# HGRN2's score products gathered into one column-tiled group, in one core's step of a hybrid retention and HGRN2 layer

## The chip, the cores and the metric

The kernel runs on one core of a Trainium2 chip. The metric is device time in microseconds; a time is the median of the runs.

## What is computed

One step of a decoder layer for two request groups that share weights: 272 prompt tokens (16 learned meta tokens and 256 of the prompt) and 8 single sample tokens with states of their own. D_MODEL is 2048, everything is float32.

```
x <- LN1(alpha*x + 0.5*SwiGLU_1(x))
x <- LN2(alpha*x + Mixer(x))        # retention and HGRN2 side by side, gated, one output projection
x <- LN3(alpha*x + 0.5*SwiGLU_2(x))

def hgrn2_chunk(S, q, k, v, logf):          # 16 heads, 128 state features
    b = cumsum(logf)
    diff = b[:, :, :, None, :] - b[:, :, None, :, :]
    decay = exp(where(causal, diff, -inf))
    A = einsum('bhid,bhjd,bhijd->bhij', q, k, decay)
    o = einsum('bhij,bhjv->bhiv', A, v) + einsum('bhid,bhdv->bhiv', q * exp(b), S)
    S_new = exp(b_last) * S + einsum('bhjd,bhjv->bhdv', k * exp(b_last - b), v)

def retention_chunk(S, q, k, v):            # 8 heads of 256, decay gamma per head
    inner = einsum('bhid,bhjd->bhij', q, k) * D
    o = einsum('bhij,bhjv->bhiv', inner, v) + einsum('bhid,bhdv->bhiv', q_dec, S)
    S_new = gamma**C * S + einsum('bhjd,bhjv->bhdv', k_dec, v)
```

In HGRN2 the decay differs for each feature, so the scores A of a chunk cannot be one plain product q k. The sample tokens take one recurrent step each and need their states (16 heads of 128 x 128 and 8 heads of 256 x 256, for each of 8 tokens) read, updated, queried and written.

## The kernel before

Activations lie transposed: features on the 128 partitions, tokens along the free dimension (280 columns, 264 without the meta tokens). Each weight matrix is streamed from memory in units of eight 128 x 128 blocks (`stream`, L170, with the load on SP's queue at L185). ScalarE casts a unit to `whi` (L188), VectorE makes the rest `wlo` (L189), and `dense` (L218) multiplies each block three times, hi by hi, hi by lo and lo by hi, in one-pass float32. Three buffers each hold `raw`, `whi` and `wlo`.

Between the two feed-forward parts stands the mixer. It runs over eight units u; a unit has two HGRN2 heads and one retention head. Per unit `project` runs ten projections of two output chunks each, 16 contraction blocks per projection, six matmuls per block. After each contraction block it calls `pump`: the two branches are generators, `mix_hg` (HGRN2) and `mix_ret` (retention), each `yield n` says after how many pumps the branch goes on, and so the branch's TensorE instructions are laid between the dense ones in an order written by hand. A branch that started first comes first within one pump. Unit u's `mix_hg` starts when its `i_h` projection is done, `mix_ret` after `v_r`; the first wait is 3 pumps, except in units 0 and 1 (20 and 46 for HGRN2, 24 for retention's unit 1). TensorE keeps that order; the instructions of the other engines and the DMA issues are put in order by a scheduler, which may put them well before the pump at which they are emitted, as far as their operands allow.

HGRN2's scores are built by levels s = 1, 2, 4, ..., 64 (`LEVELS`): at level s, the later half of each block of 2s tokens meets the earlier half. K and Q are scaled in place from level to level (`scale_k`, `scale_q`, and `join` for the products of forget gates `Ts`). Levels 1 to 8 are computed as 32 x 16 pieces (`blocks`, from the side-by-side copies Q1 and Q4 of `side_by_side`) and put into the score tile `acc` by masked copies (L834); the diagonal comes with Q1 as `own` (L828). Levels 16, 32 and 64 have products of their own (L886, L881), copied by ScalarE (L899, L894). All these products use column tiles: 32 or 64 stationary columns at a `tile_position`, so that two or four of them run side by side. A group of them takes one or two PSUM banks out of the four of `ps_m` (`mx_bank`), which also serve the transposes `pt`, `ptk` and the branches' other products.

Before the change there are five such groups per unit, at the yields L858 to L904: Q1 with the diagonal, Q4, 16, 32, 64. After the group of a level, K and Q are scaled for the next one. Q1 and Q4 lie in buffers of the tag `smh`, which the sample states (`sms`, loaded by `load`, L770, behind their broadcast `vbs` in the tag `vbh`) take afterwards. The sample states are updated at L927 and L928, and queried in a column-tiled group `pq` (L954). Retention has its own, `pqr` (L1125), which begins with a third score block of 16 columns (L1056); its first two score blocks, 256 and 144 columns wide, are full-array products into `psc`. Its own state updates are L1106 and L1112.

Of the kernel before, what the change touches and what calls it, by code (L numbers as in the profile page):

```python
# [14 lines left out]
ALU = mybir.AluOpType  # L15
# [3 lines left out]
P = 128  # L19
# [4 lines left out]
NMETA, SEQ, NS = 16, 256, 8  # L24
# [104 lines left out]
def trunk(ctx: ExitStack, tc: tile.TileContext, A, O):  # L129
# [13 lines left out]
    def mx_bank(name):  # L143
        return ps_m.tile([P, 512], F32, tag="mx", name=name)
# [135 lines left out]
    class Norm:  # L280
# [266 lines left out]
    with tc.tile_pool(name="yp", bufs=1) as yp:  # L547
# [7 lines left out]
        with tc.tile_pool(name="mp", bufs=1) as mp:  # L555
# [190 lines left out]
            def mix_hg(u, f, k, q, v):  # L746
# [18 lines left out]
                def load(h):  # L765

                    sms.append(tmp("smh", (P, NS, P), bufs=2))
                    vbs.append(tmp("vbh", (P, NS, P), bufs=2))
                    nc.sync.dma_start(vbs[h], vrow[h].partition_broadcast(P))
                    nc.sync.dma_start(sms[h], A["sg"][2 * u + h])  # L770
# [27 lines left out]

                def side_by_side(s):

                    x = tmp("Qm", (P, 3, 2 * P), tag="smh", bufs=2)
# [3 lines left out]
                    nc.scalar.copy(part(1, 2 * s), odd(2 * s))  # L805
# [5 lines left out]
                def blocks(x, s, own=None):  # L811

                    x = x.rearrange("p i (x j c) -> p i x j c", x=4, j=4)
                    for h in range(2):
                        pl = mx_bank("pl")
                        half = pl[:, : 2 * 80].rearrange("p (b c) -> p b c", b=2)
                        for b in range(2):
                            for mine in range(1 if own is None else 2):
                                for j in range(0, P, 32):
                                    at = b * P + j  # L820
                                    o, y = half[j : j + 32, b, :48].rearrange("p (i c) -> p i c", i=3), x[:, :, 2 * h + b, j // 32, :]
                                    if mine:
                                        o, y = half[j : j + 32, b, 48:], own[:, h, at : at + 32]
                                    nc.tensor.matmul(
                                        o, K[:, h, NMETA + at : NMETA + at + 32], y, start=True, stop=True, tile_position=(0, j))
                        a = acc[:, 2 * P * h : 2 * P * (h + 1)]
                        if own is not None:
                            nc.vector.tensor_tensor(  # L828
                                out=a.rearrange("p (b j c) -> p b j c", b=2, j=4),
                                in0=half[:, :, 48:].unsqueeze(2).to_broadcast([P, 2, 4, 32]),  # L830
                                in1=ident.rearrange("p (j c) -> p j c", j=4).unsqueeze(1).to_broadcast([P, 2, 4, 32]), op=ALU.mult)
                        for i, (sl, mi) in enumerate(((s, MASKS[s][0]), (2 * s, MASKS[2 * s][0]), (2 * s, MASKS[2 * s][1]))):
                            n = 16 // sl
                            nc.vector.copy_predicated(  # L834
                                a.rearrange("p (b j n t s) -> p b j n t s", b=2, j=4, t=2, s=sl)[:, :, :, :, 1, :],
                                msk[:, mi, :P].rearrange("p (b j n s) -> p b j n s", b=2, j=4, s=sl),
                                half[:, :, 16 * i : 16 * i + 16].rearrange("p b (n s) -> p b n s", s=sl).unsqueeze(2).to_broadcast([P, 2, 4, n, sl]))

                join(1)
                Q1 = side_by_side(1)  # L840
# [27 lines left out]
                for s in (4, 8):  # L868
                    scale_k(s)
                nc.gpsimd.tensor_copy(meta[:, :, :NMETA], K[:, :, :NMETA])  # L870
                scale_q(8)
                join(8)
                yield W_LEVEL + 4 + calm
                for s in LEVELS[MASKED:]:
                    pl = mx_bank("pl")
                    for h in range(2):
                        for b in range(2):
                            k0, q0, o = NMETA + b * P, b * P, (2 * h + b) * s
                            if s == 64:
                                j = 64 * b  # L880
                                nc.tensor.matmul(  # L881
                                    pl[j : j + s, h * s : (h + 1) * s], K[:, h, k0 : k0 + s], Q[:, h, q0 + s : q0 + 2 * s],
                                    start=True, stop=True, tile_position=(0, j))
                            else:
                                for j in range(0, P, 2 * s):
                                    nc.tensor.matmul(  # L886
                                        pl[j : j + s, o : o + s], K[:, h, k0 + j : k0 + j + s],
                                        Q[:, h, q0 + j + s : q0 + j + 2 * s], start=True, stop=True, tile_position=(0, j))
                    scale_k(s)
                    scale_q(s)  # L890
                    join(s)
                    if s == 64:
                        for b in range(2):
                            nc.scalar.copy(  # L894
                                acc[:s, :].rearrange("p (h b n s) -> p h b n s", h=2, b=2, s=s)[:, :, b, 1, :],
                                pl[b * s : (b + 1) * s, : 2 * s].rearrange("p (h s) -> p h s", h=2))
                    else:
                        for j in range(0, 128 // s, 2):
                            nc.scalar.copy(  # L899
                                acc[j * s : (j + 1) * s, :].rearrange("p (x n s) -> p x n s", x=4, s=s)[:, :, j + 1, :],  # L900
                                pl[j * s : (j + 1) * s, : 4 * s].rearrange("p (x s) -> p x s", x=4))
                    if s in (16, 32):
                        load(s // 32)
# [32 lines left out]
                for h in range(2):  # L936
# [63 lines left out]
            def mix_ret(u, q, k, v):  # L1000
# [52 lines left out]
                def scores(out, b):  # L1053
                    _, l0, n, nk = SCORES[b]
                    for c in range(2):
                        nc.tensor.matmul(  # L1056
                            out[:nk, :n], k[:, c, b * P : b * P + nk], q[:, c, l0 : l0 + n], start=c == 0, stop=c == 1)

                for b in range(2):
# [231 lines left out]
```

## Time and profile before

| | |
|---|---|
| median of three runs | 2581.47 us (2581.25 to 2583.45) |
| the profiled execution | 2582.39 us |
| its span, first to last instruction | 2580.6 us |
| TensorE busy | 2565.8 us, 99% |
| VectorE, ScalarE, GpSimd busy | 66%, 53%, 2% |
| the mixer, about | 750 to 1780 us of the span |
| DMA, mean over the span | 208 GB/s |

PE is the matmul side of TensorE, PEld its weight loads, which overlap. Ends of matmuls are modelled by the profiler: the step from one start to the next is the safer reading. Idle time of an engine is put down to what released it. Tile names stand as output<-inputs, with the line of the kernel.

### The profile page before, as it was taken

Reading aid. Unit: us, or ns where it says so; the run is one execution under the profiler, and the core shown is the slowest. Engines: PE = TensorE matmul, PEld = TensorE weight load, DVE = VectorE, ACT = ScalarE, POOL = GpSimd, SP = SyncE. Lnnn points to the kernel's source line nnn. Section 1 sums busy time; section 2 is a strip of 40 time slices with the busy share of each in tenths; the row PEclk is TensorE's granted clock in tenths of the full one; section 3 lists DMA queues with packets and bytes.
Section 4 is the critical chain, followed back from the end, with each engine's and each line's share of the span. In section 5 each row is a group of like instructions: output and inputs, shape, how many; then the busy total and the mean of one; then the engine's idle time right before and its main releaser. Section 6 shows DMA issues by size and latency. Waiting matters only on the chain.

```text
span 2580.6 us, 55997 instructions
## 1 busy us (share of the span) xinstructions
PE 2565.8 (99%) x23360; PEld 2540.0 (98%) x23360; DVE 1702.4 (66%) x2827; ACT 1378.0 (53%) x2146; POOL 46.4 (2%) x112
## 2 busy tenths in 40 slices
PE   9999999999999999999999999999999999999999
PEld 9999999999999999999999999999999999999998
DVE  6454454475579887777777878787985555556555
ACT  5444444444456665757575757575564444444444
POOL 0000000000000000000000000000000000000000
PEclk9999999999999999999999999999999999999999
DMA  7555555555566786767676767676666666666664
GB/s 242 182 186 184 184 187 181 188 181 184 184 200 216 248 276 208 262 211 257 213 255 216 253 220 254 215 236 195 196 186 199 196 197 195 195 194 194 196 196 149
DMA packets 156895, 536.25 MB, mean 208 GB/s; under 512 B 17952, under 2 KB 25952, under 8 KB 156640
## 3 DMA queue, kind: packets, MB, share of 16 engines
q1 hardware_dynamic: 156352, 532.37, 64.0%
q8 instruction: 183, 3.00, 0.5%
q14 instruction: 72, 0.59, 0.1%
q10 hardware_dynamic: 288, 0.29, 0.0%
HBM read 501.99 MB, written 30.61 MB: 206 GB/s over the span
## 4 chain that ended last, share of the span: by engine, by line
PE 93%; DVE 3%; DMA 2%; ACT 1%; issue 1%; SPq 0%; DVEq 0%; ACTq 0%
PE up L218 34%; PE dn L218 19%; PE pj_v_r L218 4%; PE pj_i_h L218 3%; PE pj_g_r L218 3%; PE wo L218 3%; PE pj_q_r L218 3%; PE pj_f L218 3%; PE pj_k_r L218 3%; PE pj_a_r L218 3%; PE pj_g_h L218 3%; PE pj_a_h L218 3%; PE pj_q_h L218 3%; DVE wlo L189 1%; DMA raw<-in_w_up 1%
## 5 line engine op out<-in xcount | busy, mean ns | idle before, releaser
L189 DVE TENSOR_TENSOR wlo<-raw,whi 128x1024 fp32r<-128x1024 f32 (+1 forms) x869 | 1061.8, 1222 | 762.5 <-ACT whi L188 760.8
L188 ACT CAST whi<-raw 128x1024 fp32r<-128x1024 f32 (+1 forms) x870 | 906.0, 1042 | 935.3 <-PE up L218 408.3
L218 PE MATMUL up<-xh,wlo 128*128 128x280 f32 (+1 forms) x2624 | 725.9, 280 | 1.0 <-DVE wlo L189 1.0
L218 PE MATMUL up<-xh,whi 128*128 128x280 f32 (+1 forms) x2624 | 725.7, 280 | 0.5 <-ACT whi L188 0.4
L218 PE MATMUL up<-xl,whi 128*128 128x280 f32 (+1 forms) x2624 | 725.4, 279 | 0.0
L218 PEld LDWEIGHTS up<-xh,wlo 128*128 128x128 f32 x2624 | 492.6, 189 | 1.9 <-DVE wlo L189 1.9
L218 PEld LDWEIGHTS up<-xh,whi 128*128 128x128 f32 x2624 | 492.6, 189 | 0.9 <-ACT whi L188 0.9
L218 PEld LDWEIGHTS up<-xl,whi 128*128 128x128 f32 x2624 | 492.6, 189 | 0.0
L218 PE MATMUL dn<-hh,whi 128*128 128x280 f32 (+1 forms) x1376 | 384.7, 280 | 0.0
L218 PE MATMUL dn<-hh,wlo 128*128 128x280 f32 (+1 forms) x1376 | 384.3, 279 | 0.0
L218 PE MATMUL dn<-hl,whi 128*128 128x280 f32 (+1 forms) x1376 | 384.3, 279 | 0.0
L218 PEld LDWEIGHTS dn<-hh,whi 128*128 128x128 f32 x1376 | 260.1, 189 | 0.1
L218 PEld LDWEIGHTS dn<-hl,whi 128*128 128x128 f32 x1376 | 260.1, 189 | 0.1
L218 PEld LDWEIGHTS dn<-hh,wlo 128*128 128x128 f32 x1376 | 260.1, 189 | 0.0
L218 PE MATMUL pj_g_r<-xh,whi 128*128 128x264 f32 x256 | 76.5, 299 | 0.0
L218 PE MATMUL pj_g_h<-xh,whi 128*128 128x264 f32 x256 | 74.2, 290 | 0.0
L218 PE MATMUL pj_k_r<-xh,whi 128*128 128x280 f32 x256 | 73.8, 288 | 0.0
L218 PE MATMUL pj_v_r<-xh,whi 128*128 128x280 f32 x256 | 73.4, 287 | 0.0
L218 PE MATMUL pj_v_r<-xh,wlo 128*128 128x280 f32 x256 | 72.4, 283 | 0.3 <-DVE wlo L189 0.3
L218 PE MATMUL pj_k_r<-xh,wlo 128*128 128x280 f32 x256 | 72.4, 283 | 0.0
L218 PE MATMUL pj_k_r<-xl,whi 128*128 128x280 f32 x256 | 72.3, 283 | 0.0
L218 PE MATMUL pj_v_r<-xl,whi 128*128 128x280 f32 x256 | 72.3, 283 | 0.0
(408 smaller groups left out, 5242.4 us busy)
## 6 DMA issues: line engine op xcount, KB each, us to landing
raw<-in_w_up SPq DMA_DIRECT2D x343, 512.0 KB
raw<-in_w_in SPq DMA_DIRECT2D x320, 512.0 KB
raw<-in_w_dn SPq DMA_DIRECT2D x172, 512.0 KB
smr<-in_sr SPq DMA_DIRECT2D x32, 512.0 KB
out_srs<-smr SPq DMA_DIRECT2D x32, 512.0 KB
raw<-in_w_out SPq DMA_DIRECT2D x32, 512.0 KB
smh<-in_sg SPq DMA_DIRECT2D x16, 512.0 KB
vbr<-vrd SPq DMA_DIRECT2D x32, 256.0 KB
```

The costliest lines, as they stand in the source:

```text
L188: nc.scalar.copy(hi[:, j:jn, :], raw[:, j:jn, :])
L189: nc.vector.tensor_tensor(out=lo[:, j0:j1, :], in0=raw[:, j0:j1, :], in1=hi[:, j0:j1, :].bitcast(F32), op=ALU.subtract)
L218: nc.tensor.matmul(o, w, t, start=start, stop=stop)
```

## The change

Copies are kept so that the score products of all levels can run at one place. `kept`, a tile in the tag `vbh`, holds K as it is for level 4 (`K4`) and the key halves for the levels 16 and 32; the query halves for these go into a fourth row of Q1 and Q4 (`held`). Levels 1 and 2 use the unscaled `k`. K and Q are scaled on without a group between. Then one group does Q1 with the diagonal, Q4, 16, 32 and 64, into two banks `pls`; level 64 is cut into halves of 32 stationary columns (`upper`). The masked copies (`fill`) and ScalarE's copies (`keep`) follow the group, and the two `load` calls stand right behind it. In unit 0, Q1 with the diagonal keeps its own group and banks, at its old place.

From unit 2 on, HGRN2's sample queries move from three pumps behind retention's to the same pump, by the two yields around them. In retention's score blocks the explicit tile position (0, 0) is given to the 16-column block, and the 256-column block is issued after the 144-column one.

```
-                blocks(Q1, 1, q)
+                kept = tmp("kept", (P, 4, 2 * P), tag="vbh", bufs=2)
+                K4 = kept[:, :2, :]
+                pls = [None, None]
...
+                if u == 0:
+                    for h in range(2):
+                        pls[h] = mx_bank("pl")
+                        blocks(first(h), Q1, K[:, :, NMETA:], h, q)
+                        fill(first(h), 1, h)
                 scale_q(2)
                 join(2)
                 Q4 = side_by_side(4)
                 scale_k(1)
                 scale_k(2)
-                yield 2 * W_LEVEL - 1 + calm
-                blocks(Q4, 4)
+                yield W_LEVEL + calm
+                nc.scalar.copy(K4, K[:, :, NMETA:])
                 join(4)
                 for s in (4, 8):
                     scale_k(s)
                 nc.gpsimd.tensor_copy(meta[:, :, :NMETA], K[:, :, :NMETA])
                 scale_q(8)
                 join(8)
-                yield W_LEVEL + 4 + calm
-                for s in LEVELS[MASKED:]:
-                    pl = mx_bank("pl")
...
+                yield W_LEVEL
+                held = {}
+                for i, s in enumerate((16, 32)):
+                    held[s] = kept[:, 2 + i, :], (Q1, Q4)[i][:, 3, :]
+                    nc.scalar.copy(
+                        held[s][0].rearrange("p (h n s) -> p h n s", h=2, s=s),
+                        K[:, :, NMETA:].rearrange("p h (n t s) -> p h n t s", t=2, s=s)[:, :, :, 0, :])
+                    nc.scalar.copy(held[s][1].rearrange("p (h n s) -> p h n s", h=2, s=s), odd(s))
                     scale_k(s)
                     scale_q(s)
                     join(s)
-                    yield W_LEVEL + calm
+                    yield W_LEVEL if i == 0 or u else W_LEVEL + 5
+                for h in range(2):
+                    if u or pls[0] is None:
+                        pls[h] = mx_bank("pl")
+                        blocks(first(h), Q1, k[:, :, NMETA:], h, q)
+                if u == 0:
+                    pls = [mx_bank("pl") for h in range(2)]
+                for h in range(2):
+                    blocks(second(h), Q4, K4, h)
+                tops = {16: pls[0][:, 256:320], 32: pls[0][:, 320:448], 64: pls[1][:, 256:384]}
+                for s in (16, 32):
+                    ...
+                    upper(tops[s], s, ...)
+                upper(tops[64], 64, ...)
+                scale_k(64)
+                scale_q(64)
+                join(64)
+                for h in range(2):
+                    load(h)
+                for h in range(2):
+                    if u:
+                        fill(first(h), 1, h)
+                    fill(second(h), 4, h)
+                    yield 4
+                for s in (16, 32, 64):
+                    keep(tops[s], s)
+                yield 15 if u else 10
...
-                yield 10
+                yield 7 if u > 1 else 10
                 pq = mx_bank("pq")
...
-                yield 4
+                yield 7 if u > 1 else 4
...
-                            out[:nk, :n], k[:, c, b * P : b * P + nk], q[:, c, l0 : l0 + n], start=c == 0, stop=c == 1)
-                for b in range(2):
+                            out[:nk, :n], k[:, c, b * P : b * P + nk], q[:, c, l0 : l0 + n], start=c == 0, stop=c == 1,
+                            **({"tile_position": (0, 0)} if nk <= 32 else {}))
+                for b in (1, 0):
                     scores(psc[:, SCORES[b][0] :], b)
```

More of the change, by code (lines that the diff above doesn't have):

```diff
@@ L799, in side_by_side @@
                 def side_by_side(s):
-                    x = tmp("Qm", (P, 3, 2 * P), tag="smh", bufs=2)
+                    x = tmp("Qm", (P, 4, 2 * P), tag="smh", bufs=2)
                     part = lambda i, s: x[:, i, :].rearrange("p (h n s) -> p h n s", h=2, s=s)
@@ L809, in side_by_side, with blocks @@
                     return x
-                def blocks(x, s, own=None):
-                    x = x.rearrange("p i (x j c) -> p i x j c", x=4, j=4)
+                def blocks(half, x, keys, h, own=None):
+                    x = x[:, :3].rearrange("p i (x j c) -> p i x j c", x=4, j=4)
+                    for b in range(2):
+                        for mine in range(1 if own is None else 2):
+                            for j in range(0, P, 32):
+                                at = b * P + j
+                                o, y = half[j : j + 32, b, :48].rearrange("p (i c) -> p i c", i=3), x[:, :, 2 * h + b, j // 32, :]
+                                if mine:
+                                    o, y = half[j : j + 32, b, 48:], own[:, h, at : at + 32]
+                                nc.tensor.matmul(o, keys[:, h, at : at + 32], y, start=True, stop=True, tile_position=(0, j))
@@ new lines, in fill @@
+                def fill(half, s, h):
+                    a = acc[:, 2 * P * h : 2 * P * (h + 1)]
+                    if s == 1:
+                        nc.vector.tensor_tensor(
+                            out=a.rearrange("p (b j c) -> p b j c", b=2, j=4),
+                            in0=half[:, :, 48:].unsqueeze(2).to_broadcast([P, 2, 4, 32]),
+                            in1=ident.rearrange("p (j c) -> p j c", j=4).unsqueeze(1).to_broadcast([P, 2, 4, 32]), op=ALU.mult)
+                    for i, (sl, mi) in enumerate(((s, MASKS[s][0]), (2 * s, MASKS[2 * s][0]), (2 * s, MASKS[2 * s][1]))):
+                        n = 16 // sl
+                        nc.vector.copy_predicated(
+                            a.rearrange("p (b j n t s) -> p b j n t s", b=2, j=4, t=2, s=sl)[:, :, :, :, 1, :],
+                            msk[:, mi, :P].rearrange("p (b j n s) -> p b j n s", b=2, j=4, s=sl),
+                            half[:, :, 16 * i : 16 * i + 16].rearrange("p b (n s) -> p b n s", s=sl).unsqueeze(2).to_broadcast([P, 2, 4, n, sl]))
@@ L814, in blocks, with upper @@
+                def upper(pl, s, keys, qs):
                     for h in range(2):
-                        pl = mx_bank("pl")
-                        half = pl[:, : 2 * 80].rearrange("p (b c) -> p b c", b=2)
                         for b in range(2):
[L818 to L837, printed above, removed]
+                            o = (h if s == 64 else 2 * h + b) * s
@@ new lines, in upper @@
+                            for j in range(0, P, 2 * s):
+                                y = qs(h, b, j)
+                                for i in range(0, s, 32):
+                                    r = 64 * b + i if s == 64 else j
+                                    w = min(s, 32)
+                                    nc.tensor.matmul(
+                                        pl[r : r + w, o : o + s], keys(h, b, j)[:, i : i + w], y,
+                                        start=True, stop=True, tile_position=(0, r))
@@ new lines, in keep @@
+                def keep(pl, s):
+                    if s == 64:
+                        for b in range(2):
+                            nc.scalar.copy(
+                                acc[:s, :].rearrange("p (h b n s) -> p h b n s", h=2, b=2, s=s)[:, :, b, 1, :],
+                                pl[b * s : (b + 1) * s, : 2 * s].rearrange("p (h s) -> p h s", h=2))
+                    else:
+                        for j in range(0, 128 // s, 2):
+                            nc.scalar.copy(
+                                acc[j * s : (j + 1) * s, :].rearrange("p (x n s) -> p x n s", x=4, s=s)[:, :, j + 1, :],
+                                pl[j * s : (j + 1) * s, : 4 * s].rearrange("p (x s) -> p x s", x=4))
@@ L872, in mix_hg @@
                 join(8)
-                yield W_LEVEL + 4 + calm
-                for s in LEVELS[MASKED:]:
-                    pl = mx_bank("pl")
-                    for h in range(2):
-                        for b in range(2):
[L878 to L888, printed above, removed]
+                yield W_LEVEL
+                held = {}
+                for i, s in enumerate((16, 32)):
+                    held[s] = kept[:, 2 + i, :], (Q1, Q4)[i][:, 3, :]
+                    nc.scalar.copy(
+                        held[s][0].rearrange("p (h n s) -> p h n s", h=2, s=s),
+                        K[:, :, NMETA:].rearrange("p h (n t s) -> p h n t s", t=2, s=s)[:, :, :, 0, :])
+                    nc.scalar.copy(held[s][1].rearrange("p (h n s) -> p h n s", h=2, s=s), odd(s))
                     scale_k(s)
```

20 lines of the change are left out of this document (7 added, 13 removed).

## The prediction

> **What bounds the kernel now.** I read the page from the top: engine shares, then the chain that ended last.
>
> ```profile
> span 2580.6 us, 55997 instructions
> PE 2565.8 (99%) x23360; PEld 2540.0 (98%) x23360; DVE 1702.4 (66%) x2827; ACT 1378.0 (53%) x2146; POOL 46.4 (2%) x112
> PE 93%; DVE 3%; DMA 2%; ACT 1%; issue 1%; SPq 0%; DVEq 0%; ACTq 0%
> ```
>
> TensorE is busy for 99% of the span and makes 93% of the last chain. So the change pays only where it shortens TensorE's own stream or takes away one of its few waits, and it costs only where it adds a wait there. The profiled execution took 2582.39 us, 1.8 more than its span; the median of the three timed runs is 2581.47, 0.92 lower. Sums below are made against 2582.39, and 0.92 is taken off at the end. A measurement can tell about 0.2%, 5.2 us, from no change.
>
> Next, how one column-tiled group sits in the stream. This is the TensorE timeline of unit 3, around the group `pl<-Qm,K` of the levels 4 and 8. Columns: start, us, operation, count.
>
> ```profile
> 1406.78 0.28 PE L218 MATMUL pj_k_r<-xl,whi 128*128 128x280 f32 x1
> 1406.90 0.28 PE L218 MATMUL pj_k_r<-xh,wlo 128*128 128x280 f32 x1
> 1407.11 0.55 PE L824 MATMUL pl<-Qm,K 128*32 128x48 f32 x32
> 1407.59 0.39 PE L218 MATMUL pj_k_r<-xh,whi 128*128 128x280 f32 x1
> 1407.81 0.28 PE L218 MATMUL pj_k_r<-xl,whi 128*128 128x280 f32 x1
> ```
>
> Between full-array matmuls the step is 0.12 us (1406.78 to 1406.90). Into the group it is 0.21, and from the first matmul after it to the next 0.22. Nothing is waited for; entering and leaving column tiles costs time by itself. The table by stretch gives, for unit 3, each group from the start of the last full matmul before it to the start of the second after it (us, then TensorE busy): levels 1-2 with the diagonal, 4-8, 16, 32, 64; then retention's sample queries and HGRN2's.
>
> ```profile
> 1396.65:1397.84 1.19, 1.19 (x68) 1.00 1.07 403
> 1406.90:1407.81 0.91, 0.91 (x36) 1.00 0.94 378
> 1416.15:1416.90 0.75, 0.75 (x36) 1.00 0.64 229
> 1422.31:1423.11 0.80, 0.80 (x21) 1.00 0.94 348
> 1430.63:1431.43 0.80, 0.80 (x12) 1.00 0.86 315
> 1456.77:1459.13 2.36, 2.36 (x40) 1.00 0.97 370
> 1460.93:1462.37 1.44, 1.44 (x37) 1.00 0.99 373
> ```
>
> Two of these have 32 instructions each, of 48 and of 128 columns: 0.91 and 1.44 us. The line through them is 0.53/80 = 6.6 ns per column, so at no columns 0.91 - 48 x 0.0066 = 0.59 remains, of which two full matmuls are 0.24. **A group's fixed price is about 0.35 us.** A lower end comes from the level-16 group: 0.75 less 0.24 is 0.51, and its 32 instructions need about 7 ns each to start, as these rows of retention's queries show (three `pqr<-smr,qdr` start within 0.02 us):
>
> ```profile
> 1456.98 0.24 PE L1056 MATMUL pqr<-q_r,k_r 128*16 128x16 f32 x3
> 1457.05 0.42 PE L1125 MATMUL pqr<-smr,qdr 128*32 128x256 f32 x3
> 1457.07 0.18 PE L1056 MATMUL pqr<-q_r,k_r 128*16 128x16 f32 x1
> ```
>
> That is 0.21, and leaves 0.30. I take 0.33, between 0.30 and 0.36.
>
> **The change, part by part.** Steps are counted in pumps: one follows each contraction block of a projection, six matmuls of 0.11 to 0.12 us, about 0.7 us.
>
> *Fewer groups.* In units 1 to 7 five score groups (pumps 17, 30, 42, 50, 58 after the branch starts, from unit 2 on) become one at pump 43: four fixed prices fewer in each, 28. Unit 0 keeps levels 1-2 apart: three fewer. The yields around HGRN2's queries move them for u > 1 from 94 to 91, the pump at which retention's run: six groups fewer. 37 x 0.33 = **12.2 us** (11.1 to 13.3). The products are the same; only level 64 is cut into 32-row halves, 16 instructions instead of 8, but four side by side instead of two, by 64 columns x 6.6 ns / 8 about 0.05 us a set both ways: nil. The rows above with starts 7 ns apart are what I count for an added instruction. The Trainium skill, "TensorEngine Tiling (Array Packing)", section "Instruction Overhead", puts about 60 cycles on each matmul; if that held between tiles, an estimate from its figure and the 2.4 GHz of "TensorE: Matmul & The Clock Gate" (the table at its head), 64 more instructions at 25 ns, would make the gain 1.6 us smaller. The 7 ns speak against it here.
>
> *The third score block's explicit tile position*: its 16-column products already run among 32-column ones without a break (1457.05 to 1457.07), so nothing. *The 256-column block last* reorders full-array products: nothing.
>
> *A wait that goes.* The waits of TensorE in the mixer have one large entry, in unit 1 before level 64 (its row, then TensorE's timeline, the table by stretch, and VectorE's timeline):
>
> ```profile
> PE pl L881 <- DVE Q L240: 3.3, 1, 3.3
> 944.82 0.28 PE L218 MATMUL pj_a_h<-xh,wlo 128*128 128x264 f32 x1
> 948.40 0.45 PE L881 MATMUL pl<-Q,K 128*64 128x64 f32 x8 [3.30 <-DVE Q L240]
> 949.56:952.97 3.41, 3.41 (x18) 0.51 0.97 326
> 943.54 0.42 DVE L240 TENSOR_TENSOR K<-K,T 128x256 f32<-128x256 f32 x1
> 946.64 1.27 DVE L1112 SCALAR_TENSOR_TENSOR smr<-vbr,sro,smr 128x256 f32<-128x256 f32 x3
> 947.83 0.42 DVE L240 TENSOR_TENSOR Q<-Q,T 128x256 f32<-128x256 f32 x1
> ```
>
> VectorE scales Q for level 64 only at 947.83, behind retention's state updates (L1112); TensorE stands from 944.82 to 948.40, of which 0.21 is the way into any group: 3.4 us lost. Then the granted clock is 0.51 for 3.41 us (the fourth row), another 1.7. After the change, Q and K no longer wait for the earlier score groups, since copies are kept (`K4`, `held`, and `k` itself for levels 1-2): the scaling chain can run from the branch's start, and all of it is emitted before the pump at which unit 1's joined group stands, which is also that of retention's first updates (pump 166 counted from unit 0's branch). Its work is small:
>
> ```profile
> L240 DVE TENSOR_TENSOR K<-K,T 128x272 f32<-128x272 f32 (+1 forms) x48 | 21.0, 438 | 0.2
> L805 ACT COPY Qm<-Q 128x256 f32<-128x256 f32 x16 | 6.8, 422 | 14.7 <-DVE Q L240 14.7
> L755 ACT COPY K<-k 128x544 f32<-128x544 f32 x8 | 5.1, 643 | 0.2
> ```
>
> Six scalings of K, six of Q, six joins and two products for the side-by-side blocks, 20 VectorE operations of at most 0.44 us, are 9 us; ScalarE adds one copy like L755's (0.64) and four like L805's (0.42), 2.3 us a unit. Against 40 pumps, 28 us, shared with the weight casts, that fits: **5.1 us** gained. The cover for the new copies is TensorE's stream; without it they would cost their 2.3 us a unit.
>
> *What becomes late instead.* First, PSUM. The joined group fills two of the four banks of `ps_m`, and they are read by 14 VectorE fills and 8 ScalarE copies afterwards, no longer spread over 40 pumps:
>
> ```profile
> L834 DVE COPY_PREDICATED acch<-msk,pl 128x128 f32<-128x128 uint8 x96 | 27.7, 379 | 0.1
> L828 DVE TENSOR_TENSOR acch<-pl,ident 128x256 f32<-128x256 f32 x16 | 7.0, 437 | 1.0 <-PE pl L824 1.0
> L899 ACT COPY acch<-pl 16x64 f32<-16x64 f32 (+1 forms) x48 | 10.6, 221 | 8.6 <-PE pl L886 8.2
> L189 DVE TENSOR_TENSOR wlo<-raw,whi 128x1024 fp32r<-128x1024 f32 (+1 forms) x869 | 1061.8, 1222 | 762.5 <-ACT whi L188 760.8
> 1417.00:1436.00 19.00, 19.00 (x179) 18.54 (x178) 14.28 (x29) 14.26 (x36) 1.50 (x3) 1.00 0.56 179
> ```
>
> 12 x 0.38 + 2 x 0.44 = 5.4 us, with the three scalings of level 64 about 6.4, and a cast of 1.2 us every 2.7 besides: done 8 to 10 us after the group. The copies overwrite what the fills wrote, so they follow: 8 x 0.22 and a cast, 2 to 3 us more. Retention's transposes come at pumps 51, 52, 54 and 55, that is 5.5 to 9 us after the group. The first two take the free banks; the third can take the first's, which is copied out at once; the fourth may meet a bank still held. Ends: nothing, since only one of the four banks is missing, and 2 us in each of units 2 to 7, 12 us. VectorE and ScalarE are idle a quarter of that stretch (14.28 and 14.26 of 19.00 us in the last row; columns: length, PE, PEld, DVE, ACT, POOL, clock, DMA share, GB/s), so I take near the low end, 1.5 us in all.
>
> Second, DMA. Q1 and Q4 lie in the buffers of the sample states, so SP's loads of these follow the last reader. Now they are issued at 1397.67 and 1408.38, right behind the groups:
>
> ```profile
> 1397.67 0.33 SPq L770 DMA_DIRECT2D smh<-in_sg  x1
> 1408.38 1.69 SPq L770 DMA_DIRECT2D smh<-in_sg  x1
> 830.00:850.00 20.00, 18.78 (x224) 17.71 (x224) 16.15 (x37) 15.96 (x28) 1.81 (x4) 1.00 0.88 295
> 850.00:872.00 22.00, 22.00 (x210) 20.59 (x209) 18.69 (x47) 15.09 (x37) 1.43 (x3) 1.00 0.89 284
> ```
>
> Afterwards both, and one broadcast into the buffer that `kept` took, come behind the one group: 1.5 MB at once, with the weight loads queued behind them on SP. In units 2 to 7 the DMA share there is 0.56, so there is room. In unit 0 the group falls at about 850, into a share of 0.89 at 284 GB/s; 1.5 MB over 22 us are 68 GB/s more, 352, below the 403 seen above, so a weight block may be a little late; the stretch before gets emptier by as much. Ends: a gain of 1.2 us (TensorE's idle time in 830:850) and a loss of 3; I take a loss of 0.5.
>
> **Sum**: 12.2 + 5.1 - 1.5 - 0.5 = 15.3. 2582.39 - 15.3 = 2567.1 by the profiled execution, **2566 us** as a median.
>
> **The rivals.** (1) *The wait moves to the banks.* The transposes at pumps 54 and 55 wait 1.5 us in each of units 2 to 7: 9 us, less the 1.5 already counted, 2574. For it: 22 evacuations in a row where there were five portions. Against: idle time in both engines, and only one bank of four missing.
> (2) *Slower: the same wait, long enough to lower the clock.* The one wait of 3.3 us on the page was followed by 3.4 us at half clock. If fills and copies take over 12 us, each of six units waits 3.5 us and loses 1.7 more at half clock: 31 us against 17.3 gained, 2582.39 + 13.9 - 0.92 = 2595. It decides from 2.9 us a unit, where the gain is gone. For it: casts go between the fills on VectorE, in order, and retention's own evacuations begin at pump 51. The Trainium skill, "PSUM - Partial Sum Buffer", section "PSUM bank collisions raise a hardware error", says that two engines must not touch one bank and 32-partition quadrant at once; so levels 16 to 64 cannot be copied out beside the fills of their bank. No row of before shows a bank shared in this way.
> (3) *Joining saves nothing*: each change of block shape inside the group, and from HGRN2's queries to retention's, costs the fixed price again. Then only unit 1's wait goes: 2582.39 - 5.1 + 2.0 - 0.92 = 2578. Against it stand the three rows with 16 and 32 columns mixed.
>
> **How the numbers follow.** Forecast 0.68; rival 1 0.13, most of it still faster by over 5.2 us; rival 2 0.12; rival 3 0.07, nearly all within 0.2%. So faster 0.79, same 0.09, slower 0.12. The low end takes 13.3 + 5.1 + 1.2 = 19.6 without new waits: 2562. The high end takes in rivals 1 and 3: 2578; what is left out is rival 2 and little else.
>
> **What would show it.** In the profile after: between two full matmuls one block of some 176 products per unit, with one step of about 0.2 us into it and one out; `pq` and `pqr` products adjacent from unit 2 on; mixer stretches of units 2 to 6 shorter by 1.6 us each; no TensorE wait on Q in unit 1 and no stretch at clock 0.5 there. Wrong would be: waits of TensorE at the `pt` lines or at `pl` with ScalarE or VectorE as releaser, weight casts waiting for `raw` behind the joined group in units 0 and 1, or steps of 0.2 us inside the group.

## The result, and the profile after

The change made the kernel slower. Medians: 2601.32 us (2599.12 to 2606.83, six runs) against 2582.27 us (2581.25 to 2583.45, six runs), ratio 1.0077 with the interval 1.0064 to 1.0090. That is 19 us the wrong way, where 16 the other way were forecast, and outside the range.

The page of the changed kernel, the lines that answer to the first three of before (span, engines, chain that ended last):

```profile
span 2598.9 us, 56199 instructions
PE 2562.9 (99%) x23424; PEld 2537.6 (98%) x23424; DVE 1703.5 (66%) x2827; ACT 1389.4 (53%) x2186; POOL 34.1 (1%) x112
PE 81%; DVE 7%; ACT 6%; DMA 3%; issue 2%; POOL 0%; SPq 0%; DVEq 0%; ACTq 0%
```

TensorE's busy time fell by 2.9 us while the span grew by 18.3, and its share of the last chain fell from 93% to 81%. Its own stream got shorter, and it now waits for others. First the stream: TensorE's timeline of unit 5 (start, us, operation, count; the prediction calls this place unit 3, but the loads of the states just before it, at 1397.67 and 1408.38 us of before, are the eleventh and twelfth of sixteen, two to a unit, so it is unit 5 counted from 0), then the table by stretch from the last dense product before the group to the second after it, for the joined scores and for the joined queries.

```profile
1424.72 0.28 PE L218 MATMUL pj_v_r<-xh,wlo 128*128 128x280 f32 x1
1424.93 0.29 PE L821 MATMUL pl<-Qm,k 128*32 128x48 f32 x8
...
1426.41 0.41 PE L847 MATMUL pl<-Q,K 128*32 128x64 f32 x14
1426.74 0.39 PE L218 MATMUL pj_v_r<-xh,whi 128*128 128x280 f32 x1
1426.97 0.28 PE L218 MATMUL pj_v_r<-xl,whi 128*128 128x280 f32 x1
```

```profile
1424.72:1426.97 2.25, 2.25 (x165) 2.02 (x164) 0.70 (x3) 0.00 (x0) 0.00 (x0) 1.00 0.52 153
1469.01:1472.26 3.25, 3.25 (x73) 2.21 (x72) 1.94 (x5) 1.31 (x2) 0.00 (x0) 1.00 0.87 257
```

One step of 0.21 us leads in (1424.72 to 1424.93), one of 0.23 out, none between. Without the two dense steps of 0.12, the joined group takes 2.01 us; the five groups of before took 4.45 less five times 0.24, 3.25. The joined queries take 3.25 where the two took 2.36 and 1.44 with one pair of dense steps more: about 0.3 less. So 1.24 and 0.3 us a unit are saved, as forecast (1.32 and 0.33).

Now the new waits. TensorE's waits over the mixer, the largest that unit after unit repeats (us in total, times, longest):

```profile
PE pt L1063 <- ACT v L684: 11.0, 6, 2.1
PE pj_g_h L218 <- DVE wlo L189: 7.1, 8, 1.2
PE pt L1070 <- ACT acch L859: 1.9, 5, 0.4
```

In each of units 2 to 7 retention's first transpose, `pt` at pump 51, waits 1.5 to 2.1 us for ScalarE's copy of `v` (L684), an operation that the prediction never mentions. Before, ScalarE's timeline of unit 5 had the two copies of `v`, and the scaling of the sample states (L927) 12 us behind the second:

```profile
1420.97 0.39 ACT L684 COPY v<-pj_v_r 128x280 f32<-128x280 f32 x1 [1.63 <-PE pj_v_r L218]
1422.21 0.40 ACT L685 COPY v<-pj_v_r 128x280 f32<-128x280 f32 x1
1434.22 0.99 ACT L927 ACTIVATE smh<-smh,fs 128x128 f32<-128x128 f32 x3
```

After, from SP's queue, from the chain of waits of unit 5 in order of time (start, us, what), and from ScalarE's timeline:

```profile
1426.40 0.33 SPq L770 DMA_DIRECT2D smh<-in_sg  x1
```

```profile
1426.40 4.95 DMA smh<-in_sg
1431.74 0.97 ACT smh L968 x3
1432.71 0.93 ACT whi L188
1433.67 0.39 ACT v L684
```

```profile
1431.43 1.28 ACT L968 ACTIVATE smh<-smh,fs 128x128 f32<-128x128 f32 x4 [2.75 <-DMA smh<-in_sg]
```

The chain is to be read downwards. The load of the sample states goes out at 1426.40, with the group's last read of Q1, and lands 4.95 us later. ScalarE has the scaling of these states (L968, L927 of before) at the head of its queue and stands 2.75 us for the load; a weight cast and the copies of `v` stand behind it. The copies come at 1433.67, and TensorE's transpose has waited for them.

Two things had to meet. The loads come late, because the joined group is now the last reader of their buffers. And the scaling stands ahead of the copies of `v`: its factor `fs` takes the buffer of `T64`, which the last link of the chain of scalings releases. That link moved from pump 58 to pump 43, and the scheduler moved the state scaling forward with it. DMA was not short of room:

```profile
1425.00:1437.00 12.00, 10.49 (x234) 10.21 (x235) 8.58 (x26) 6.55 (x16) 0.76 (x2) 1.00 0.71 244
```

In unit 5 the share is 0.71 at 244 GB/s and the clock 1.00. VectorE (8.58 of 12.00 us) and ScalarE (6.55) are far from full: `v` is late by the order of ScalarE's work and not by its amount. The Trainium skill, "TensorE: Matmul & The Clock Gate", gives ScalarE and VectorE strict first-in-first-out queues (the table at its head, row "Engine queue depth"); the copies of `v` held at 1433.67 behind a scaling that waits agree with it.

In one of the six units the wait also lowered the clock. In unit 6 the transpose waited 2.1 us, and from 1566.1 us on TensorE ran at half clock for 3.4 us (stretch: length, PE, clock, DMA share, GB/s), which is 1.7 us more:

```profile
1566.10:1569.50 3.40, 3.40 (x18) 0.50 0.53 159
```

Unit 1's wait on Q is gone, and so is the half clock there, 1.00 against the 0.51 of before:

```profile
944.00:952.00 8.00, 7.23 (x61) 6.79 (x61) 6.08 (x17) 6.69 (x21) 0.00 (x0) 1.00 0.82 290
```

But in units 0 and 1 other waits came. TensorE's waits between 840 and 970 us, the largest:

```profile
PE pj_g_h L218 <- DVE wlo L189: 1.9, 2, 1.2
PE por L1182 <- ACT osr L1173: 1.3, 1, 1.3
PE por L741 <- ACT kth L964: 1.0, 1, 1.0
```

The second of them hangs on unit 0's late load by the same kind of chain: the load lands, ScalarE scales the states, and its copy of unit 1's `v` and then `osr` come late:

```profile
855.44 6.43 DMA smh<-in_sg
863.84 0.39 ACT v L667
869.49 0.38 ACT osr L1173
```

### The profile page after: what moved, and what is told of

It is laid out like the page before. It is cut to its first block, busy times and chain, and to the rows that moved or that the text cites. A ratio compares the mean times of both kernels' runs of the same rounds, so it can differ in the third digit from the quotient of the medians.

```text
span 2598.9 us, 56199 instructions
## 1 busy us (share of the span) xinstructions
PE 2562.9 (99%) x23424; PEld 2537.6 (98%) x23424; DVE 1703.5 (66%) x2827; ACT 1389.4 (53%) x2186; POOL 34.1 (1%) x112
## 4 chain that ended last, share of the span: by engine, by line
PE 81%; DVE 7%; ACT 6%; DMA 3%; issue 2%; POOL 0%; SPq 0%; DVEq 0%; ACTq 0%
PE up L218 35%; PE dn L218 18%; PE wo L218 3%; DVE wlo L189 3%; PE pj_k_r L218 3%; PE pj_f L218 3%; ACT whi L188 2%; PE pj_v_r L218 2%; PE pj_g_r L218 2%; PE pj_g_h L218 2%; PE pj_a_h L218 2%; PE pj_a_r L218 2%; PE pj_q_r L218 2%; PE pj_q_h L218 2%; DMA smh<-in_sg 2%
## 5 line engine op out<-in xcount | busy, mean ns | idle before, releaser
L218 PE MATMUL pj_g_h<-xh,wlo 128*128 128x264 f32 x256 | 71.6, 280 | 7.1 <-DVE wlo L189 7.1
```

What stands on the lines that cost most here:

```text
L218: nc.tensor.matmul(o, w, t, start=start, stop=stop)
```

## The experiments

The dense products are the same in all kernels, so two traces can be laid side by side: the start of a dense product in one less its start in the other, and how this difference grows. Growth is read from the one profiled execution of each kernel, the median from all of its runs. The table gives, beside median and ratio, its growth over units 0 and 1 (about 837 to 999 us of before) and its mean growth per unit over five units after that (1079 to 1720 us). Differences of 1.5 us in the first column say nothing: after, e1_smr, e8_early and e10_both have the same instructions in units 0 and 1, and stand there at +0.3 to +1.8 (1.7 of e10_both's is half clock behind unit 0, which the other three do not have there).

| kernel | median, us | ratio to before | units 0, 1 | per later unit |
|---|---|---|---|---|
| after | 2601.32 | 1.0077 (1.0064 to 1.0090) | +1.0 | +3.04 |
| e1_smr | 2586.10 | 1.0014 (1.0005 to 1.0023) | +0.4 | +0.68 |
| e2_gate | 2599.38 | 1.0064 (1.0051 to 1.0078) | +9.0 | +1.33 |
| e4_split | 2589.02 | 1.0028 (1.0017 to 1.0039) | -1.1 | +1.45 |
| e5_queries | 2580.07 | 0.9994 (0.9985 to 1.0002) | +0.3 | -0.42 |
| e6_late | 2588.02 | 1.0023 (1.0013 to 1.0034) | +7.5 | +0.18 |
| e7_three | 2592.81 | 1.0046 (1.0029 to 1.0063) | +3.0 | +1.21 |
| e8_early | 2606.12 | 1.0091 (1.0076 to 1.0106) | +0.3 | +4.43 |
| e10_both | 2580.09 | 0.9989 (0.9980 to 0.9999) | +1.8 | -0.67 |
| e11_unit0 | 2573.64 | 0.9965 (0.9951 to 0.9978) | -4.0 | -0.67 |

The theory: the loss of units 2 to 7 is ScalarE's order, a scaling that waits for a late load ahead of the copies of `v`. The rivals: the added evacuations, or the burst of 1.5 MB on the DMA queues.

**e1_smr: the changed kernel with loads early again.** From unit 2 on, Q1, Q4 and the copies lie in retention's buffers, so the state buffers are free early.

```
-  x = tmp("Qm", (P, 4, 2 * P), tag="smh", bufs=2)
+  x = tmp("Qm", (P, 4, 2 * P), tag="smr" if u > 1 else "smh", bufs=4 if u > 1 else 2)
-  kept = tmp("kept", (P, 4, 2 * P), tag="vbh", bufs=2)
+  kept = tmp("kept", (P, 4, 2 * P), tag="smr" if u > 1 else "vbh", bufs=4 if u > 1 else 2)
```

> The changed kernel, with Q1, Q4 and kept of the units 2 to 7 in retention's four state buffers, which are idle at that time, so that HGRN2's sample states can be loaded before the joined group. Theory A (the loads, held back by the joined group's reads, keep ScalarE standing at the scaling of the states, and with it the copies of v that retention's transposes need): the wait of the first transposes (1.7 to 2.4 us a unit) and most of what follows it go, about 4 us in each of six units: 2601 - 25 = 2576, between 2572 and 2584. Theory B (22 evacuations of two banks in a row make VectorE and ScalarE late): the loads do not matter, the waits at the transposes stay, 2596 to 2603. Theory C (the scaling of the states stands ahead of v in ScalarE's order and delays it by its own 2.4 us, whenever the data lands): half of the wait stays, 2586 to 2594.

15 of the 19 us came back, with the same products, copies and evacuations. TensorE's waits over the mixer, the ones to compare with after:

```profile
PE pj_g_h L218 <- DVE wlo L189: 8.9, 8, 1.3
PE pt L1070 <- ACT acch L859: 0.6, 4, 0.2
```

The wait on `v` is not in the list any more, although part of the scaling still stands ahead of the copies of `v` (ScalarE, unit 5):

```profile
1422.03 2.15 ACT L968 ACTIVATE smh<-smh,fs 128x128 f32<-128x128 f32 x7
1424.20 0.39 ACT L684 COPY v<-pj_v_r 128x280 f32<-128x280 f32 x1
```

The total missed theory A by 2 us and lies at the low end of theory C's range; but C kept half of the wait on `v`, and none of it is left, so the wait speaks for A. The late loads are worth 3.04 - 0.68 = 2.36 us a unit in the changed kernel. What remains is above all a cast that comes late at `pj_g_h`, 1.2 us a unit in the six later units.

**e2_gate: loads still late, but the scaling held back.** The factor `fs` is multiplied by a one that is made from the transposed K (`kt`), so the scaling can't stand ahead of that.

```
-  nc.gpsimd.tensor_copy(fs, fk[:, 0])
...
+  one = tmp("one", (P, 1))
+  nc.gpsimd.tensor_scalar(out=one, in0=kt[:, 0, 0:1], scalar1=1.0, scalar2=1.0, op0=ALU.min, op1=ALU.max)
+  nc.vector.tensor_scalar(out=fs, in0=fk[:, 0], scalar1=one, scalar2=None, op0=ALU.mult)
```

> The changed kernel, with the scaling of HGRN2's sample states made to wait for the copy of the transposed K at pump 66 (a one made from it is multiplied into fs); buffers and loads as in the changed kernel. Theory A and theory C: nothing stands ahead of v on ScalarE any more, the first transposes do not wait, units 0 and 1 gain as well: 2570 to 2580. Theory B: the waits at the transposes stay, 2596 to 2603. New risk in all: the states are ready later and the query group at pump 91 waits.

On the wait in question it answers clearly: with the loads as late as in the changed kernel, the wait on `v` is gone too, and the step per unit falls from +3.04 to +1.33. ScalarE copies `v` as soon as TensorE has it:

```profile
1432.13 0.39 ACT L684 COPY v<-pj_v_r 128x280 f32<-128x280 f32 x1 [1.63 <-PE pj_v_r L218]
```

The total, 2599.38, lies in theory B's range all the same, because units 0 and 1 lose 9.0 us here, part of it at half clock (0.83 on average over 866 to 876 and over 960 to 975 us). That the scaling, now late itself, causes the waits there is argued, not shown. The largest of TensorE's waits:

```profile
PE por L1186 <- DVE sc L255: 7.8, 2, 5.8
```

**e4_split: the kernel before with the five score groups cut in two, by head.** It prices a group by itself.

```
-  blocks(Q1, 1, q)
+  blocks(Q1, 1, q, (0,))
+  yield 1
+  blocks(Q1, 1, q, (1,))
...
+                        if h == 0:
+                            yield 1
```

> The kernel before, with each of the five score groups cut in two by head, one pump apart: the same products, 40 groups more. If a group costs TensorE 0.33 us by itself: 2582 + 13.2 = 2595, between 2594 and 2597; each half group in the table by stretch is 0.30 to 0.36 us longer than its products need. If the price were a matter of waits and not of the group, or is hidden: under 2587.

The total is 6.8 us above before, half of what 40 groups at 0.33 give. By place it is another picture: +1.45 us per later unit, five added groups, 0.29 each, at the low end of the forecast's 0.30 to 0.36. The rest of the difference lies in units 0 and 1, where shifting the stream by a few pumps took away two waits on casts, 1.3 us in all, and made the wait on Q shorter, 1.5 us instead of 3.3.

**e5_queries: the kernel before with only the sample queries joined.**

```
-  yield 10
+  yield 7 if u > 1 else 10
...
-  yield 4
+  yield 7 if u > 1 else 4
```

> The kernel before, with HGRN2's sample queries moved to retention's pump from unit 2 on and nothing else. All theories: six groups fewer, 2582.3 - 2.0 = 2580.3, between 2579.8 and 2581; no new wait. If the joining of the queries costs something (two banks taken at once, states needed three pumps earlier): 2582 or more.

2.2 us below before, ratio 0.9994 with an interval that holds 1. The step per unit is -0.42 by the mean of five and -0.33 by their median: the price of one group once more.

**e6_late: the kernel before with only the loads late.** Two one-column products in the level-32 group read Q1 and Q4 once more, into columns that nothing uses; both loads are issued behind it.

```
+  if s == 32:
+      for i, x in enumerate((Q1, Q4)):
+          nc.tensor.matmul(pl[:32, 4 * s + i : 4 * s + i + 1], K[:, 0, NMETA : NMETA + 32], x[:, 2, 2 * P - 1 :],
+                           start=True, stop=True, tile_position=(0, 0))
...
-  if s in (16, 32):
-      load(s // 32)
+  if s == 32:
+      for h in range(2):
+          load(h)
```

> The kernel before, but both loads of the sample states are held back until the level-32 group (two one-column products there read Q1 and Q4 once more), so they land some 5 us later, about 25 us later than now and about 6 us ahead of the state scaling. Theory (ScalarE's order: late loads cost only where the scaling stands in ScalarE's queue ahead of the copies of v): the scaling still comes behind the copies of v here, so 2582 to 2583 us. Rival (the burst itself, 1.5 MB at once just ahead of retention's transposes, takes the bandwidth of the weight loads or of retention's loads): about 2 us in each of units 2 to 7, 2592 to 2596 us.

The total missed by 5 us, and the table says where: the later units lose 0.18 each, so there late loads alone cost next to nothing, as long as the scaling stands behind the copies of `v`. In unit 5 the load goes out on SP's queue at 1430.94, and on ScalarE the scaling (L933) comes 12 us behind the second copy of `v`:

```profile
1430.94 0.33 SPq L770 DMA_DIRECT2D smh<-in_sg  x1
```

```profile
1430.13 0.40 ACT L685 COPY v<-pj_v_r 128x280 f32<-128x280 f32 x1
1442.23 0.99 ACT L933 ACTIVATE smh<-smh,fs 128x128 f32<-128x128 f32 x3
```

That speaks against the burst as the cause. Units 0 and 1 lose 7.5 us, in a profiled execution that is the slowest of the eight runs, 3.3 us above their median. TensorE's waits between 864 and 876 us, then a row of ScalarE, and the stretch from 870 (length, PE, PEld, DVE, ACT, POOL, clock, DMA share, GB/s):

```profile
PE por L741 <- DVE fk L760: 3.2, 1, 3.2
PE por L1146 <- ACT sc L724: 1.7, 1, 1.7
```

```profile
861.44 1.57 ACT L933 ACTIVATE smh<-smh,fs 128x128 f32<-128x128 f32 x5 [3.56 <-DMA smh<-in_sg]
```

```profile
870.00:876.00 6.00, 2.86 (x12) 2.71 (x12) 3.65 (x10) 3.72 (x8) 0.00 (x0) 0.69 0.86 264
```

In unit 0 the scaling stands at the head of ScalarE's queue and waits 3.56 us for its load, at a DMA share of 0.86 after it. That the two waits of TensorE a few us later, and the clock after them (0.69), follow from it is argued from their place. A part of the 7.5 us is not the loads': the wait on Q is 3.3 us as before, but 6.8 us at half clock follow it here (954 to 961 us) and 3.4 before, 1.7 us more.

**e8_early: the changed kernel with the joined group nine pumps earlier, at pump 34.**

```
-  yield W_LEVEL
+  yield 3 if u > 1 else W_LEVEL
...
-  yield W_LEVEL if i == 0 or u else W_LEVEL + 5
+  yield 3 if u > 1 else W_LEVEL if i == 0 or u else W_LEVEL + 5
...
-  yield 15 if u else 10
+  yield 24 if u > 1 else 15 if u else 10
```

> The changed kernel with the joined group, from unit 2 on, at pump 34 instead of 43; what follows stays at its pumps. The loads stay behind the group. Theory (ScalarE stands for the loads with the copies of v behind it): the loads land about 6 us earlier, the scaling is through before the copies of v, TensorE's wait of 11 us at retention's first transpose goes; 2586 to 2590 us. Rival (22 evacuations from two banks are what is late): the burst is only moved, and VectorE and ScalarE still meet retention's own with the same work; 2597 to 2601 us.

The expectation was wrong by some 18 us, and my number for the theory with it: it came out above the rival's. The loads do come earlier, but so does everything that releases the scaling, and the scheduler now puts all of it ahead of `v`. TensorE's largest wait, then ScalarE's timeline of unit 5:

```profile
PE pt L1063 <- ACT v L684: 15.1, 6, 2.9
```

```profile
1427.17 1.86 ACT L968 ACTIVATE smh<-smh,fs 128x128 f32<-128x128 f32 x6 [3.49 <-DMA smh<-in_sg]
...
1433.95 1.86 ACT L968 ACTIVATE smh<-smh,fs 128x128 f32<-128x128 f32 x6
1435.84 0.39 ACT L684 COPY v<-pj_v_r 128x280 f32<-128x280 f32 x1
```

ScalarE stands 3.49 us for the load and then has sixteen scalings, eight copies and two casts to do before `v`, at 1435.84. e10_both, below, has the same work ahead of `v` with its loads early, and no wait on `v`. So the mechanism is the theory's, and the remedy was none: earlier by nine pumps is of no use where the waiter moves forward with what it waits for. The waits of 2.7 to 2.9 us in units 4 to 7 were each followed by half clock, for 3.4 us and once for 6.8, those of 1.7 and 2.0 us in units 2 and 3 were not; so the +4.43 hold about 1.7 us a unit of clock.

**e10_both: e1_smr and e8_early together.** Loads early, group at pump 34.

> As e1_smr (Q1, Q4 and the copies in retention's buffers, loads early), and the joined group at pump 34 from unit 2 on. If what e1_smr still loses per unit (1.3 us at pj_g_h on a cast that is late, 0.4 at a transpose) comes from the evacuations and the state scaling falling together with retention's evacuations, these go: 2576 to 2580 us, faster than the kernel before. If it comes from the added copies and would be there wherever the group stands: 2585 to 2587 us.

2580.09 us, a hair faster than before (the interval ends at 0.9999). Against e8_early only the loads differ: 4.43 + 0.67 = 5.1 us a unit, with the clock that its waits cost. Against e1_smr only the place differs: 0.68 + 0.67 = 1.35 us a unit; the late cast at `pj_g_h` is gone from the later units (8.9 us in eight waits there, 1.9 in two here). Standing ahead of `v` does no harm by itself: ScalarE still waits up to 3.5 us for the scaling's factor, but at a place where the casts have time. Its waits from 1227 to 1820 us, and TensorE's over the mixer, one row each:

```profile
ACT smh L968 <- POOL fs L950: 14.0, 4, 3.5
```

```profile
PE pj_g_h L218 <- DVE wlo L189: 1.9, 2, 1.2
```

**e7_three: e1_smr with Q1's and Q4's blocks back in groups of their own** (pumps 17 and 28), only 16, 32 and 64 joined at pump 43.

```
-  if u == 0:
-      for h in range(2):
-          pls[h] = mx_bank("pl")
+  for h in range(2):
+      pls[h] = mx_bank("pl")
...
+  pls = [mx_bank("pl") for h in range(2)]
+  for h in range(2):
+      blocks(second(h), Q4, K4, h)
+      fill(second(h), 4, h)
```

> As e1_smr, but Q1's and Q4's blocks keep groups of their own at pumps 17 and 28, with their masked copies right behind; only the levels 16, 32 and 64 are joined, at pump 43. By the price of a group (0.33 us), 15 groups more than e1_smr cost 5 us. If the burst of masked copies behind the joined group makes the casts late, 6 to 10 us come back: 2581 to 2585 us. If the early state scaling does it, nothing comes back: 2590 to 2592 us.

2592.81: nothing came back. The masked copies are spread out again here, and the step per unit is +1.21, of which two added groups are about 0.6; what is left is e1_smr's 0.68. By place it is less plain. TensorE's waits of units 2 to 7:

```profile
PE pj_g_h L218 <- DVE wlo L189: 3.4, 6, 0.7
PE pt L1055 <- ACT v L684: 2.7, 6, 0.4
PE pj_g_r L218 <- DVE wlo L189: 2.0, 6, 0.6
```

In e1_smr these were 7.0, nothing and 0.4. The late cast at `pj_g_h` did get half as long, and two other waits took its place. So the burst of masked copies is no loss that spreading them wins back, but that it has no part in the late cast is not shown. Whether the rest of that wait is the state scaling among retention's evacuations stays open too, since e10_both moved the scaling and the evacuations together.

**e11_unit0: e10_both with unit 0 in the form of before.** Five groups there, loads right behind Q1's and Q4's.

```
+  if u == 0:
+      for h in range(2):
+          pl = mx_bank("pl")
+          half = pl[:, : 2 * 80].rearrange("p (b c) -> p b c", b=2)
+          blocks(half, Q1, K[:, :, NMETA:], h, q)
+          fill(half, 1, h)
...
+          if s in (16, 32):
+              load(s // 32)
+          yield W_LEVEL + calm
+  else:
```

> As e10_both, but unit 0 keeps the form of the kernel before: five score groups, loads right behind Q1's and Q4's. Theory: in unit 0 the late loads cost TensorE some 5 us (steps of 1.3, 1.1 and 2.7 us at 846, 855 and 870 us in e10_both, less about 1 for its groups), and these go: 2575 to 2577 us, faster than both kernels. Rival (the waits there come from the joined queries and scores of unit 1 or differ from run to run): 2579 to 2581 us as e10_both.

2573.64 us (2572.14 to 2573.87), ratio 0.9965 (0.9951 to 0.9978): faster than both kernels, 8.7 us below before and 1.4 below the low end expected. Units 0 and 1 now gain 4.0 us where e10_both lost 1.8; 1.7 of these 5.8 us is the half clock at 872 us in e10_both's execution.

## Why the prediction was wrong

**Fewer groups, 12.2 us: right.** 0.29 us a group by e4_split, 0.33 to 0.42 by e5_queries, and 1.24 us for four by the joined group's own stretch. The trace gave this price well without any experiment. In that group some 160 products start within 1.81 us, 11 ns each. The Trainium skill's 60 cycles for each matmul ("TensorEngine Tiling (Array Packing)", section "Instruction Overhead"), 25 ns by the prediction's estimate, would be 4 us if they were paid one after another over the whole group, and the group is shorter than that. The products go to column tiles in turn, though, mostly four, so by an estimate from the 11 ns one tile starts a product every 45 ns, and whether the 25 ns hold within a tile is not shown by any run here.

**A wait that goes, 5.1 us: right as a term, not as a gain.** Both the wait on Q and the half clock are gone. In units 0 and 1 together the changed kernel still lost 1.0 us, since three smaller waits came and unit 0 paid for its late loads. With unit 0 left alone, the gain is there (-4.0).

**Banks late, 1.5 us: small as forecast.** The fourth transpose waits in five of the six units for ScalarE's copies of levels 16 and 32 (L859) out of the joined group's bank, as the prediction has it, 1.9 us in all; dense products there come about 0.6 us later, 3.1 us over the five units. That is twice the 1.5 and within the ends of 0 and 12.

**DMA, 0.5 us: here it failed.** The step read: "In units 2 to 7 the DMA share there is 0.56, so there is room." There was room, and the loads took only 4.95 us. But the step priced a transfer by bandwidth and never asked who waits for it and what stands behind the waiter. The price of the moved loads is 2.36 us in each of six units (after less e1_smr), 14 us. Unit 0's new form costs about 5 more (after less e11_unit0, 1.0 + 4.0), where the prediction's end for its loads was 3; that it is the loads there, and not the rest of the form, is argued from the chain at 855 us and from e6_late.

**The step that is missing.** The prediction says that the scaling chain "can run from the branch's start", and counts it as good. It did not follow the chain to its end: the state scaling hangs on it through the buffer of `T64`, and it moved 15 pumps forward in ScalarE's queue, ahead of `v`. e1_smr, e2_gate and e6_late show the pair: late loads with the scaling behind `v` cost 0.18 us a unit, early loads with the scaling ahead have no wait on `v`, and both together wait. The place of the group among retention's evacuations costs 1.35 us a unit more (e1_smr less e10_both). Of the 1.40 us a unit that was forecast (1.65 for five groups less 0.25 for banks) e10_both gets 0.67. The other 0.7 stands in its trace as waits of 4.7 us over units 2 to 7: 3.0 in three places at `pj_v_r` for which the profile names no releaser, 1.2 on `ends`, the rest on casts and masked copies; it was not followed further. So from -1.40 to the measured +3.04, 4.44 us a unit, are 2.36 of loads and order, 1.35 of place and 0.73 of this rest.

**The rivals.** Rival 2 had the sign and nearly the time (2595), but not its place, and that is luck: the waits that count are at the first transpose and not the fourth, and for `v` and not for a bank. Of its mechanism, a wait that lowers the clock, one unit of six shows something in the profile (1.7 us in unit 6). What the text named as a sign of failure, "waits of TensorE at the `pt` lines", is what came. Rival 1's wait came at 0.4 us a unit instead of 1.5, rival 3 did not come.

## What to carry to other kernels

A DMA that moves is priced by the instruction that waits for it, by the place of that instruction in its engine's queue, and by what stands behind it; a free share of bandwidth (0.71 here) says nothing about that. Where a scheduler orders the queues, taking away a dependency moves work forward that nobody meant to move: follow each shortened chain to its last reader. In this kernel the joined group paid once its inputs lay in buffers that nothing else was waiting for, and once it stood away from the next burst of evacuations (e10_both, e11_unit0).

## What the runs showed of the hardware

The clock did not answer to waits by their length alone. In e4_split a wait of 1.5 us was followed by 3.4 us at half clock (948.5 us); in the changed kernel five waits of 1.5 to 2.0 us were not, and one of 2.1 was. e10_both and the changed kernel have the same two waits in unit 0, 1.3 and 1.0 us with 1.2 us from one product to the other. Behind them the clock was 0.50 in e10_both (first row: length, PE, clock, DMA share, GB/s) and 1.00 in the changed kernel (second row):

```profile
872.10:875.50 3.40, 3.40 (x18) 0.50 0.96 361
872.00:876.00 4.00, 4.00 (x37) 1.00 0.99 368
```

What decides was not looked into. It also varies between executions: the profiled one of the changed kernel was granted 0.999 on average, the five others 0.996 to 0.998. So a wait of 1.5 to 3 us cost here what it lasted, or 1.7 us more, or 3.4 more (after 2.9 us in e8_early), and one profile shows one case of it.
